# Norms that travel by rows: column sums, a power on GpSimd and a spread through device memory

## The chip, the cores and the metric

The kernel runs on one core of a Trainium2 chip. The metric is the device time of one execution in microseconds (us). Three executions of the kernel before took 1455.49, 1453.04 and 1453.77 us, so the median is 1453.77 us. A core has five engines with a queue each: TensorE (PE, matrix products; PEld is its loading of weights), VectorE (DVE), ScalarE (ACT), GpSimd (POOL) and SyncE (SP, which only issues transfers). ScalarE and GpSimd can issue transfers too. Each queue is worked off in order, and an instruction that waits holds up those behind it.

## The reference

The program is a two-layer encoder over x (512 positions of 1024 features) and a memory of 256 positions. Everything is float32.

```python
def rms_norm(x, gain):
    y = x32 * lax.rsqrt(jnp.mean(x32 * x32, axis=-1, keepdims=True) + RMS_EPS)
    return (y * gain).astype(x.dtype)
...
for layer in range(DEPTH):
    xn = rms_norm(x, mix_norm[layer])
    mixed = fox_diff_mixer(xn, ...) if layer % 2 == 0 else mlstm_mixer(xn, ...)
    x = x + mixed
    x = x + memory_cross_attention(rms_norm(x, xattn_norm[layer]), rms_norm(mem, mem_norm[layer]), ...)
    x = x + conv_ffn(rms_norm(x, ffn_norm[layer]), ...)
return rms_norm(x, final_norm)
```

Layer 0's mixer has eight heads of forgetting attention, whose logits get the running sum of a gate per key position, and four heads of differential attention, whose outputs are each normed (`rms_norm(d_out, subln)`). Layer 1's mixer is an mLSTM with four heads; a running maximum and its exponential per position enter each head, and each head's output is normed. So besides the three norms of x in each layer, the last norm and two norms of the memory, there are eight norms of heads. The two norms of the memory differ only in their gains.

## The kernel before, in words

Activations lie with features on the 128 partitions and the 512 positions along the free axis, in eight blocks. A product in full precision is made of three matmuls (`mm3`, L289 to L291, and L351 to L353 where positions become rows) on a high part in the format fp32r and a low rest. The high part is made by ScalarE (`split`, L282) and the rest by VectorE (L279). Weights come in blocks of 128x1024 by SyncE's queue into three "raw" buffers and are split into three pairs of buffers. Projections collect in four accumulator banks ("acc"); four more PSUM banks ("s" and "w", two of each) serve the rest.

A norm's gain is put on x before the projection, and its root per position after it, when the accumulator is emptied. The root is made like this. ScalarE and VectorE sum the squares of all blocks into one tile of 128x512 (`squares`). `rsqrt_cols` sums over the partitions with eight small instructions on TensorE (L417; in the feed-forward part L1218), so that position p of a group lies on partition p. `rsqrt` makes the inverse root on VectorE with a first guess from the bits and three Newton steps (L426 to L432). `bcast_cols` spreads it to all 128 partitions: VectorE multiplies a unit matrix by the high and the low part of the roots (L446), two matmuls with ones put the result into a bank (L452), and ScalarE copies it to the tile "rb" (L456), or VectorE reads it there. Gate rows of single heads are split (`split_rows`) and spread by a matmul with a selecting matrix (`bcast_row`, L612).

The order of the mixers and of cross-attention is made by a planner (`Plan`), a list by priority with a resource for each kind of buffer, and that of the feed-forward part by `Sched`, with due times; both work with assumed costs. The framework below takes their order as a priority, schedules again by its own estimates, and adds the waits. At the end of each mixer stand fill blocks (`p_fill`: two blocks of the next part's keys, each with a bank), then the output projection (`p_out`): eight projections of eight steps, where step k needs the k-th block of the mixer's output. Cross-attention (`xattn`) follows with queries from x and keys and values from the memory; its query evacuation (L1057) multiplies by rb. The feed-forward part (`ffn_steps`) begins with four pairs of plain up-projections, whose evacuation (L1317) multiplies by rb, and four blocks of transforms of x on VectorE (L1251 to L1259) for the later pairs, which are multiplied with seven products in place of eight. The last part (`finish`) norms in two halves and writes the output.

Of the kernel before, what the change touches and what calls it, by code (L numbers as in the profile page):

```python
# [16 lines left out]
P = 128  # L17
# [12 lines left out]
WARM = 12  # L30
DECAY_AT = 90.0
# [48 lines left out]
class Plan:  # L80
# [17 lines left out]
    def run(self):  # L98
        todo = sorted(self.items, key=lambda i: (i.prio, i.n))
        eng, t = self.eng, self.t  # L100
        while todo:
# [29 lines left out]
            for e, d in pick.chain:  # L131
                u = max(u, eng[e]) + d
                eng[e] = u
                u += 0.06
# [103 lines left out]
class Builder:  # L238
# [130 lines left out]
    def p_norm(self, pl, state, n, done, scale, eps, fin, deps=(), prio=None, after=0.0, fdeps=(), chain=(("A", 0.5),)):  # L369

        st = {}

        def one():
            st["r"] = self.rsqrt_cols(state["sq"], n, scale, eps)

        def two():
            fin(st["r"], self.bcast_cols(st["r"], n, *done))

        a = pl.add(one, 0.4 * n / 512, deps, prio, take=("s",), free=("s",), chain=(("D", 2.3),), after=after)
        return pl.add(two, 0.5 * n / 512, [a, *fdeps], prio, take=("s",), free=("s",), chain=chain)  # L380

    def x_norm(self, pl, prio=0, after=0.0, deps=()):
        def fin(r, rb):
            self.r, self.rb = r, rb

        return self.p_norm(pl, self.state, SEQ, (self.sp, "rb", 1), 1.0 / DM, EPS, fin, deps, prio, after)

# [32 lines left out]
    def rsqrt(self, ps, nt, scale, eps):  # L420
        nc = self.nc
        z = self.til(self.sp, "z", (P, 4))[:, :nt]
        zh = self.til(self.sp, "zh", (P, 4))[:, :nt]
        y = self.til(self.sp, "y", (P, 4))[:, :nt]
        a = self.til(self.sp, "a", (P, 4))[:, :nt]
        nc.vector.tensor_scalar(out=z, in0=ps[:, 0 : 2 * nt : 2], scalar1=float(scale), scalar2=float(eps), op0=ALU.mult, op1=ALU.add)  # L426
        nc.vector.tensor_scalar(out=y.bitcast(I32), in0=z.bitcast(I32), scalar1=-0.5, scalar2=1597463007.0, op0=ALU.mult, op1=ALU.add)
        nc.vector.tensor_scalar(out=zh, in0=z, scalar1=-0.5, scalar2=None, op0=ALU.mult)
        for _ in range(3):
            nc.vector.tensor_tensor(out=a, in0=y, in1=y, op=ALU.mult)  # L430
            nc.vector.tensor_tensor(out=a, in0=a, in1=zh, op=ALU.mult)
            nc.vector.scalar_tensor_tensor(out=y, in0=a, scalar=1.5, in1=y, op0=ALU.add, op1=ALU.mult)  # L432
        return y

    def bcast_cols(self, r, n, pool=None, tag=None, bufs=2):
# [7 lines left out]
        ps = self.bank("b")  # L443
        for i, part in enumerate((rh, rl)):
# [7 lines left out]
            nc.tensor.matmul(banked(ps[:, :n]), self.onesr[:], alternate(dg[:, :nt, :].rearrange("p a b -> p (a b)")), start=i == 0, stop=i == 1)  # L452
        if pool is None:
            return restored(ps[:, :n])
        out = self.til(pool, tag, (P, n), bufs=bufs)
        nc.scalar.copy(folded(out[:, :n]), restored(ps[:, :n]))  # L456
# [47 lines left out]
    def xnorm(self, state):  # L504
        self.r = self.rsqrt_cols(state["sq"], SEQ, 1.0 / DM, EPS)
        self.rb = self.bcast_cols(self.r, SEQ, self.sp, "rb", 1)

# [7 lines left out]
    def constants(self):  # L515
# [8 lines left out]
        self.selc = cp.tile([P, 12], F32, name="selc")  # L524
        nc.vector.tensor_tensor(out=self.selc[:, 0:8], in0=self.ident[:, 0:8], in1=self.ident[:, 32:40], op=ALU.add)
        nc.vector.tensor_tensor(out=self.selc[:, 8:12], in0=self.ident[:, 64:68], in1=self.ident[:, 96:100], op=ALU.add)
# [67 lines left out]
    def split_rows(self, pool, *rows):  # L594

        t = pool.tile([P, SEQ], F32R, name=self.nm("rows"))
        self.nc.gpsimd.memset(t[:].bitcast(F32), 0.0)
        for n, v in enumerate(rows):
            h = v.shape[0]
            hi, lo = t[64 * n : 64 * n + h, :], t[64 * n + 32 : 64 * n + 32 + h, :]  # L600
            self.nc.scalar.copy(hi, v)
            part = self.til(self.sp, "sqt")
            self.nc.scalar.copy(part[:h, :], hi.bitcast(F32))
            self.nc.vector.tensor_tensor(out=lo, in0=v, in1=part[:h, :], op=ALU.subtract)
        return t

    def bcast_row(self, rows, c):

        ps = self.bank("b")
        s = self.til(self.sp, "sel", (P, P), F32R)  # L610
        self.nc.vector.tensor_copy(s[:], self.selc[:, c : c + 1].to_broadcast([P, P]))
        self.nc.tensor.matmul(banked(ps[:]), s[:], alternate(rows[:]), start=True, stop=True)  # L612
        return restored(ps[:])

# [42 lines left out]
    def p_soft(self, pl, st, s, i, bias, deps, prio):  # L657
# [6 lines left out]
        def score():  # L664
# [6 lines left out]
            e = res["e"] = self.x[self.turns % 8]  # L671
            self.turns += 1
# [22 lines left out]
    def turn(self, e, i, pt):  # L695

        nc = self.nc
        ps = self.bank("t")
# [45 lines left out]
    def mix0(self):  # L744
        nc, t, tc = self.nc, self.t, self.tc
        with tc.tile_pool(name="mix0", bufs=1, reuse_waits="tile") as mp:
# [5 lines left out]
            NTA = 3  # L752
# [6 lines left out]
            pl = Plan(s=2, w=2, e=8, qk=2, pt=3, ta=NTA, v=2, wt=3)  # L759
            self.state = {}  # L760
            self.turns = 0
            self.xh, self.xl = [None] * 8, [None] * 8
            self.x = [self.xp.tile([P, SEQ], F32, name=f"x{k}") for k in range(KB8)]
            gw = self.gate_weights(t["gate0"], 8, [(0, 0, 40, 8)])
# [34 lines left out]

            def spread():  # L800
                self.rb = self.bcast_cols(self.r, SEQ, self.sp, "rb", 1)

            norm = pl.add(inverse, 0, [last], 0.5, free=("s",), chain=(("D", 2.3),))
            norm = pl.add(spread, 0.5, [norm], 0.5, take=("s",), free=("s",), chain=(("A", 0.5),))
# [9 lines left out]
            def decays():  # L814
                f = self.log_sigmoid_sum(rows["z"], 8, mp, "ta", "tb", "tmp", NTA)
                rows["f"] = self.split_rows(mp, f)

            g = self.p_gate(pl, lambda: gw, 40, gates, xk, [norm], 1)
            g = pl.add(decays, 0, [g], 1, take=("ta", "ta"), free=("ta", "ta"), chain=(("A", 1.0), ("D", 4.0), ("A", 1.0), ("D", 0.6)), after=DECAY_AT)
# [4 lines left out]
            for h in range(4):  # L824
# [7 lines left out]
                for i in range(4):  # L832
# [5 lines left out]
                    def both(r1=r1, r2=r2, n=n):  # L838
# [3 lines left out]
                        nc.vector.scalar_tensor_tensor(out=e1[:, :n], in0=e1[:, :n], scalar=s1[:, 2:3], in1=e2[:, :n], op0=ALU.mult, op1=ALU.add)  # L842

# [19 lines left out]
                def scaled(r, rb, h=h, o=o):  # L863
                    q = o["o"]
                    nc.vector.scalar_tensor_tensor(out=folded(q[:]), in0=folded(q[:]), scalar=sub8, in1=rb, op0=ALU.mult, op1=ALU.mult)
# [6 lines left out]
            for p_ in range(4):  # L872
# [8 lines left out]
                for s in range(2):  # L881
# [9 lines left out]
                    b = pl.add(spread, MM, [g, *qk], p + SOFT_PRIO, take=("s", "ta"), free=("s",), chain=(("A", 0.5),))  # L891
# [22 lines left out]
                pl.add(lambda: None, 0, ss, p + SOFT_PRIO, free=("qk", "ta", "ta"))  # L914
# [29 lines left out]
    def p_memory(self, pl, layer, at, step, order=()):  # L944
# [3 lines left out]
        self.memr = mp.tile([P, 2], F32, name=f"memr{layer}")  # L948
# [12 lines left out]
        for k in range(KB8):  # L961

            def prep(k=k):
# [4 lines left out]
                self.squares(k, raw, MEM, state)  # L968
# [865 lines left out]
```

## Time and profile before

| What | Value |
|---|---|
| median of three executions | 1453.77 us |
| the profiled execution, whole | 1455.27 us |
| its span in the profile | 1453.5 us |
| TensorE busy | 1427.1 us |
| VectorE busy | 1193.3 us |
| ScalarE busy | 801.7 us |
| GpSimd busy | 57.9 us |
| granted TensorE clock, mean | 0.998 |
| read from device memory, written | 168.21 MB, 2.10 MB |

The span runs from the first to the last instruction of the program; the whole time includes what lies around it. In rows of groups, the two numbers behind the bar are the group's busy time in us and the mean of one instruction in ns; then follows the idle time of the engine just before them and what ended it. In rows in order of time, the first number is the start in us and the second the length. Matmuls overlap with the ones behind them: a row's length is longer than the time from its start to the next one's. In the chain, pieces are cut so that they don't overlap. A row of a transfer has its size and the median time from issue to landing.

### The profile page before, as it was taken

Reading aid. Unit: us, or ns where it says so; the run is one execution under the profiler, and the core shown is the slowest. Engines: PE = TensorE matmul, PEld = TensorE weight load, DVE = VectorE, ACT = ScalarE, POOL = GpSimd, SP = SyncE. Lnnn points to the kernel's source line nnn. Section 1 sums busy time; section 2 is a strip of 40 time slices with the busy share of each in tenths; the row PEclk is TensorE's granted clock in tenths of the full one; section 3 lists DMA queues with packets and bytes.
Section 4 is the critical chain, followed back from the end, with each engine's and each line's share of the span. In section 5 each row is a group of like instructions: output and inputs, shape, how many; then the busy total and the mean of one; then the engine's idle time right before and its main releaser. Section 6 shows DMA issues by size and latency. Waiting matters only on the chain.

```text
span 1453.5 us, 22202 instructions
## 1 busy us (share of the span) xinstructions
PE 1427.1 (98%) x8330; PEld 1267.4 (87%) x8330; DVE 1193.3 (82%) x2255; ACT 801.7 (55%) x1345; POOL 57.9 (4%) x100
## 2 busy tenths in 40 slices
PE   9999999999999999999999999999999999999998
PEld 7888868899889999899888788889988899999987
DVE  7778886766689999999778868676667999999975
ACT  7767574444466555545456734444445655555544
POOL 0000120000001000000000100000000000000000
PEclk9999999999999999999999999999999999999999
DMA  5222304324248666542332232323323756564322
GB/s 200 88 73 73 102 32 158 117 86 131 87 138 196 172 156 166 145 131 66 94 103 87 74 102 78 111 91 127 117 87 123 200 156 168 159 160 133 89 70 80
DMA packets 60796, 171.74 MB, mean 118 GB/s; under 512 B 6673, under 2 KB 6673, under 8 KB 60689
## 3 DMA queue, kind: packets, MB, share of 16 engines
q1 hardware_dynamic: 55072, 152.43, 32.3%
q0 software_dynamic: 4608, 16.78, 6.9%
q8 instruction: 65, 1.06, 0.3%
q10 hardware_dynamic: 1008, 1.12, 0.2%
q14 instruction: 43, 0.34, 0.1%
HBM read 168.21 MB, written 2.10 MB: 117 GB/s over the span
## 4 chain that ended last, share of the span: by engine, by line
PE 68%; DVE 22%; issue 4%; ACT 4%; DMA 1%; POOL 0%; DVEq 0%; ACTq 0%; POOLq 0%
PE acc L289 13%; PE acc L291 13%; PE acc L290 13%; DVE wl L279 5%; DVE c L1281 4%; PE w L289 3%; PE w L290 3%; PE w L291 3%; PE acc L351 2%; PE s L289 2%; PE acc L352 2%; PE acc L353 2%; PE s L291 2%; PE s L290 2%; PE w L1621 1%
## 5 line engine op out<-in xcount | busy, mean ns | idle before, releaser
L289 PE MATMUL acc<-xh,wh 128*128 128x512 f32 (+1 forms) x832 | 293.3, 353 | 0.1
L291 PE MATMUL acc<-xh,wl 128*128 128x512 f32 (+1 forms) x832 | 289.1, 347 | 1.3 <-DVE wl L279 1.3
L290 PE MATMUL acc<-xl,wh 128*128 128x512 f32 (+1 forms) x832 | 289.0, 347 | 0.0
L279 DVE TENSOR_TENSOR wl<-raw,wh 128x1024 fp32r<-128x1024 f32 (+2 forms) x201 | 240.6, 1197 | 39.3 <-ACT wh L282 35.8
L282 ACT CAST wh<-raw 128x1024 fp32r<-128x1024 f32 (+2 forms) x137 | 140.3, 1026 | 156.2 <-PE acc L290 96.7
L291 PEld LDWEIGHTS acc<-xh,wl 128*128 128x128 f32 x832 | 158.2, 190 | 16.8 <-DVE wl L279 1.6
L289 PEld LDWEIGHTS acc<-xh,wh 128*128 128x128 f32 x832 | 158.2, 190 | 15.4 <-ACT v L1393 0.3
L290 PEld LDWEIGHTS acc<-xl,wh 128*128 128x128 f32 x832 | 158.2, 190 | 15.0
L1281 DVE SCALAR_TENSOR_TENSOR c<-hs,vec,c 128x512 f32<-128x512 f32 x176 | 129.3, 750 | 5.1 <-ACT c L1274 4.6
L289 PE MATMUL w<-ah,wh 128*128 128x512 f32 x304 | 115.6, 380 | 0.0
L291 PE MATMUL w<-ah,wl 128*128 128x512 f32 x304 | 115.3, 379 | 0.0
L290 PE MATMUL w<-al,wh 128*128 128x512 f32 x304 | 115.3, 379 | 0.0
L1274 ACT ACTIVATE c<-hs,vec 128x512 f32<-128x512 f32 x88 | 69.7, 812 | 56.5 <-DVE hs L1419 49.2
L291 PEld LDWEIGHTS w<-ah,wl 128*128 128x128 f32 x304 | 57.5, 189 | 8.1
L289 PEld LDWEIGHTS w<-ah,wh 128*128 128x128 f32 x304 | 57.7, 190 | 7.2 <-ACT c L1289 0.5
L290 PEld LDWEIGHTS w<-al,wh 128*128 128x128 f32 x304 | 57.7, 190 | 6.7
L289 PE MATMUL acc<-mem,wh 128*128 128x256 f32 (+1 forms) x192 | 60.3, 314 | 0.0
L291 PE MATMUL acc<-mem,wl 128*128 128x256 f32 (+1 forms) x192 | 59.8, 311 | 0.0
L290 PE MATMUL acc<-mem,wh 128*128 128x256 f32 (+1 forms) x192 | 59.6, 311 | 0.0
L512 DVE TENSOR_TENSOR x<-w,x 128x512 f32<-128x512 f32 x72 | 49.5, 688 | 9.1 <-PE w L291 9.1
L1183 ACT CAST wh<-dr 128x512 fp32r<-128x512 f32 x64 | 39.4, 615 | 31.1 <-PE w L290 15.3
L512 DVE TENSOR_TENSOR x<-acc,x 128x512 f32<-128x512 f32 x32 | 22.1, 691 | 40.4 <-PE acc L291 40.4
(373 smaller groups left out, 3758.5 us busy)
## 6 DMA issues: line engine op xcount, KB each, us to landing
raw<-in_up_dram SPq DMA_DIRECT2D x56, 512.0 KB, 3.3
dr<-in_down_dram SPq DMA_DIRECT2D x64, 256.0 KB, 2.9
sa<-in_up_dram SPq DMA_DIRECT2D x32, 512.0 KB, 4.2
sa<-in_up_dram POOLq DMA_DIRECT2D x32, 512.0 KB, 5.5
raw<-in_xk_dram SPq DMA_DIRECT2D x16, 512.0 KB, 3.3
raw<-in_wo_dram SPq DMA_DIRECT2D x16, 512.0 KB, 3.2
raw<-in_xq_dram SPq DMA_DIRECT2D x16, 512.0 KB, 3.3
raw<-in_xv_dram SPq DMA_DIRECT2D x16, 512.0 KB, 3.2
```

Source lines behind the costliest of these rows:

```text
L279: self.nc.vector.tensor_tensor(out=lo, in0=v, in1=hi.bitcast(F32), op=ALU.subtract)
L282: self.nc.scalar.copy(hi, v)
L289: mm(out, wh, xh, start=first, stop=False, skip_group_check=parts)
L290: mm(out, wh, xl, start=False, stop=False, skip_group_check=parts)
L291: mm(out, wl, xh, start=False, stop=last, skip_group_check=parts)
L351: mm(ps, xh[k][:, ts], wh, start=(k == 0), stop=False)
L352: mm(ps, xh[k][:, ts], wl, start=False, stop=False)
L353: mm(ps, xl[k][:, ts], wh, start=False, stop=(k == 7))
L512: self.nc.vector.tensor_tensor(out=x, in0=restored(ps[:]), in1=x, op=ALU.add)
L1183: nc.scalar.copy(st["wh"][:, :cols], st[tag][:, :cols])
L1274: nc.scalar.activation(st["c_"][:, j, :], hs()[:, j, 2:514], AF.Identity, scale=self.col("cw", (layer * 3 + 2) * 44 + blk), bias=self.col( ...
L1281: nc.vector.scalar_tensor_tensor(out=c, in0=hs()[:, j, n : n + 512], scalar=w, in1=c, op0=ALU.mult, op1=ALU.add)
```

## The change

Twelve norms (both of cross-attention, both of the feed-forward parts, four heads of differential attention, four of the mLSTM) take a new way, `p_row_norm`:

1. ScalarE casts the summed squares and VectorE subtracts, which gives a high and a low part (`row_parts`).
2. Two matmuls of 512 columns with the ones as weights sum over the partitions (`row_sums`); every partition then holds the whole row. ScalarE writes one partition's row, scaled and with epsilon added.
3. ScalarE's queue copies the row from one partition to 128 partitions of four values (`row_turned`).
4. GpSimd raises it to the power -0.5 and its queue stores it to a tile in device memory (`row_root`).
5. SyncE's queue loads that row into all 128 partitions (`row_spread`).

The other norms keep their way, but their root too is a power on GpSimd in place of the Newton steps, and the products with the unit matrix become a step of their own. The gate rows are stored to device memory and loaded into 128 partitions, one transfer for each forgetting head and two for each mLSTM head; the mLSTM's second row is put through the exponential before that, on four partitions. The memory's roots are made in layer 0 only, stored, and loaded again for layer 1, whose squares of the memory are dropped. Buffers: "ta" goes from three to two, the gate rows of layer 0 get three of their own ("fb"), those of layer 1 two each, and the eight tiles that hold attention scores are taken from a list of free ones. The planner gets assumed costs for transfers.

```diff
+ROW_DMA, SPREAD_DMA = 2.5, 3.1
...
+    def row_parts(self, sq):
+        hi, lo = (self.til(self.sp, "sqt", dtype=F32R) for _ in range(2))
+        self.split(hi[:], lo[:], sq[:])
+        return hi, lo
+
+    def row_sums(self, parts, scale, eps):
+        ps = self.bank("b")
+        for i, part in enumerate(parts):
+            self.nc.tensor.matmul(banked(ps[:]), self.onesr[:], alternate(part[:]), start=i == 0, stop=i == 1)
+        row = self.til(self.sp, "sqt")
+        self.nc.scalar.activation(folded(row[0:1, :]), restored(ps[0:1, :]), AF.Copy, scale=float(scale), bias=float(eps))
+        return row
+
+    def row_turned(self, row):
+        z = self.til(self.sp, "z", (P, 4))
+        self.nc.scalar.dma_start(z[:], row[0:1, :].rearrange("o (p j) -> o p j", j=4))
+        return z
+
+    def row_root(self, z):
+        y = self.til(self.sp, "y", (P, 4))
+        self.nc.gpsimd.tensor_tensor(out=y[:], in0=z[:], in1=self.power[:], op=ALU.pow)
+        d = self.til(self.dp, "roots", (1, SEQ))
+        self.nc.gpsimd.dma_start(d[:].rearrange("o (p j) -> (o p) j", j=4), y[:])
+        return d
+
+    def row_spread(self, d, to):
+        rb = self.til(*to)
+        self.nc.sync.dma_start(rb[:], d[0:1, :].to_broadcast([P, SEQ]))
+        return rb
...
     def rsqrt(self, ps, nt, scale, eps):
...
-        nc.vector.tensor_scalar(out=y.bitcast(I32), in0=z.bitcast(I32), scalar1=-0.5, scalar2=1597463007.0, op0=ALU.mult, op1=ALU.add)
-        nc.vector.tensor_scalar(out=zh, in0=z, scalar1=-0.5, scalar2=None, op0=ALU.mult)
-        for _ in range(3):
-            nc.vector.tensor_tensor(out=a, in0=y, in1=y, op=ALU.mult)
-            nc.vector.tensor_tensor(out=a, in0=a, in1=zh, op=ALU.mult)
-            nc.vector.scalar_tensor_tensor(out=y, in0=a, scalar=1.5, in1=y, op0=ALU.add, op1=ALU.mult)
+        nc.gpsimd.tensor_tensor(out=y, in0=z, in1=self.power[:, :nt], op=ALU.pow)
...
+    def spread_row(self, rows, c, tile):
+        self.nc.sync.dma_start(tile[:], rows[c : c + 1, :].to_broadcast([P, SEQ]))
...
-            NTA = 3
+            NTA = 2
...
-            pl = Plan(s=2, w=2, e=8, qk=2, pt=3, ta=NTA, v=2, wt=3)
+            pl = Plan(s=2, w=2, e=8, qk=2, pt=3, ta=NTA, fb=3, v=2, wt=3)
...
-                f = self.p_norm(pl, sq, SEQ, (), 1.0 / P, EPS, scaled, [w], p + SOFT_PRIO, chain=(("D", 0.66),))
+                f = self.p_row_norm(pl, sq, 1.0 / P, EPS, (mp, "hrb", (P, SEQ), F32, 1), scaled, [w], p + SOFT_PRIO, chain=(("D", 0.66),))
...
                     def spread(h=h, fb=fb):
-                        fps = self.bcast_row(rows["f"], h)
-                        fb["b"] = self.til(mp, "ta", bufs=NTA)
-                        nc.scalar.copy(folded(fb["b"][:]), fps)
+                        fb["b"] = self.til(mp, "fb", bufs=3)
+                        self.spread_row(rows["d"], h, fb["b"])
...
+            self.memd = self.til(self.dp, "memroots", (1, MEM), bufs=1)
+            nc.sync.dma_start(self.memd[:], rb[0:1, :])
+
+        def again():
+            self.memrb = self.til(mp, "memrb", (P, MEM), bufs=1)
+            nc.sync.dma_start(self.memrb[:], self.memd[0:1, :].to_broadcast([P, MEM]))
...
-            norm = self.x_norm(pl, 0, deps=self.xdone[7])
+            norm = self.x_row_norm(pl, 0, self.xdone[7])
...
+            a = add("ACT", 0.52, parts_, (), at)
+            a = add("DVE", 0.6, low, [a], at)
+            a = add("PE", 0.43, sums, [a], at, [("s", st)])
+            a = add("ACT", 0.6, row, [a], at, (), [("s", st)], ROW_DMA)
+            a = add("POOL", 1.05, root, [a], at, (), (), ROW_DMA)
+            return add("SP", 0.1, spread, [a], at, (), (), SPREAD_DMA)
...
-                gt["rows"] = self.split_rows(mp, mx, mt)
+                nc.scalar.activation(mt, mt, AF.Exp, scale=-1.0)
+                gt["rows"] = mx, mt
                 gt["u"] = zi
+                gt["d"] = [self.til(self.dp, n, (H, SEQ), bufs=1) for n in ("mx", "emt")]
+                for d, v in zip(gt["d"], gt["rows"]):
+                    nc.gpsimd.dma_start(d[:], v)
...
-                f = self.p_norm(pl, st, SEQ, (), 1.0 / 256, 0.0, scaled, ns, p + 3, fdeps=oe, chain=(("D", 1.32),))
+                f = self.p_row_norm(pl, st, 1.0 / 256, 0.0, (mp, "hrb", (P, SEQ), F32, 1), scaled, ns, p + 3, fdeps=oe, chain=(("D", 1.32),))
```

More of the change, by code (lines that the diff above doesn't have):

```diff
@@ L367, in p_proj_tok, with p_norm @@
         ]
[L369 removed]
+    def p_norm(self, pl, state, n, done, scale, eps, fin, deps=(), prio=None, after=0.0):
         st = {}
@@ L376, in two @@
         def two():
[L377 to L380 removed]
+            fin(st["r"], self.spread_cols(st["d"], n, *done))
+        a = pl.add(one, 0.9 * n / 512, deps, prio, take=("s",), free=("s",), chain=(("D", 0.1), ("G", 1.05)), after=after)
+        b = pl.add(lambda: st.update(d=self.diag_cols(st["r"], n)), 0, [a], prio, chain=(("D", 0.2 + 1.2 * n / 512),))
@@ L442, in bcast_cols @@
         self.sub(rl, r, rh)
-        ps = self.bank("b")
-        for i, part in enumerate((rh, rl)):
+        out = []
+        for part in (rh, rl):
             dg = self.til(self.sp, "sqt", dtype=F32R)[:].rearrange("p (a b) -> p a b", b=P)
@@ L592, in log_sigmoid_sum @@
         return f
[L594 to L613, printed above, removed]
+    def spread_row(self, rows, c, tile):
+        self.nc.sync.dma_start(tile[:], rows[c : c + 1, :].to_broadcast([P, SEQ]))
     def q_parts(self, ps):
@@ L967, in prep @@
                 raw = raws[k // 4][:, k % 4 * MEM : k % 4 * MEM + MEM]
-                self.squares(k, raw, MEM, state)
+                if layer == 0:
+                    self.squares(k, raw, MEM, state)
                 self.gained(k, raw, self.col("mem", layer * 8 + k), hi, lo)
-            done[k] = [pl.add(prep, 0, (), 0, after=at + step * (k // 4) + (k % 4) * 0.7, order=[last], chain=(("A", 0.71), ("D", 0.4)), load=(("D", 0.4),))]
+            done[k] = [pl.add(prep, 0, (), 0, after=at + step * (k // 4) + (k % 4) * 0.7, order=[last], chain=(("A", 0.71), ("D", 0.4)), load=(("D", 0.4),) if layer == 0 else ())]
         def fin(r, rb):
```

146 lines of the change are left out of this document (89 added, 57 removed).

## The prediction

> **What bounds the kernel now.** I read the page's busy line and chain first, then the waits, then busy time by stage for the first feed-forward part, then single windows around the places where a norm is made.
>
> ```profile
> span 1453.5 us, 22202 instructions
> PE 1427.1 (98%) x8330; PEld 1267.4 (87%) x8330; DVE 1193.3 (82%) x2255; ACT 801.7 (55%) x1345; POOL 57.9 (4%) x100
> PE 68%; DVE 22%; issue 4%; ACT 4%; DMA 1%; POOL 0%; DVEq 0%; ACTq 0%; POOLq 0%
> ACT wh L282 <- PE acc L290: 96.7, 40, 5.0
> core 0: us, PE busy (x) PEld busy (x) DVE busy (x) ACT busy (x) POOL busy (x), PEclk, DMA share, GB/s
> 433.00:485.00 52.00, 51.10 (x346) 47.55 (x345) 51.99 (x82) 31.44 (x49) 5.27 (x6) 1.00 0.75 189
> ```
>
> TensorE is busy for 1427.1 of 1453.5 us at a granted clock of 1.00: a matmul that goes away shortens the run, and a norm that comes late costs only where TensorE has nothing else. The fourth line says that the casts of the weights wait for TensorE to give back a buffer, so loaded weights lie ready. The row by stage shows the exception: from 433 us VectorE too is full (51.99 of 52.00), so VectorE work that starts late at the head of the feed-forward part stays late.
>
> **TensorE work.**
>
> ```profile
> L417 PE MATMUL s<-ones,sq x40: 167/251/272, 167.7 to 1445.0; 128*128 128x2 f32 x40
> L417 PE MATMUL s<-ones,tb x32: 168/251/252, 99.8 to 156.5; 128*128 128x2 f32 x32
> L417 PE MATMUL s<-ones,hsq x32: 168/251/251, 814.0 to 920.9; 128*128 128x2 f32 x32
> 267.33 1.01 PE s L417 x8
> 920.37 0.80 PE s L417 x8
> L452 PE MATMUL s<-sqt,ones 128*128 128x512 f32 x28 | 11.4, 429 | 2.9 <-DVE sqt L446 2.5
> 925.40 0.48 PE s L452
> 926.32 0.22 PE s L452
> L612 PE MATMUL s<-rows,sel 128*128 128x512 f32 x16 | 6.1, 410 | 0.1
> 780.66 0.59 PE L612 MATMUL s<-rows,sel 128*128 128x512 f32 x2
> 781.09 0.38 PE L289 MATMUL acc<-xh,wh 128*128 128x512 f32 x1
> ```
>
> Matmuls overlap, so their price is from start to start. Eight column sums take 0.80 to 1.01 us; I take 0.9, and twelve norms lose 12 x 0.9 = 10.8. Two gate rows occupy 780.66 to 781.09, 0.215 each: 16 x 0.215 = 3.4. A spread matmul takes 0.22 when nothing waits, and 2.9 us of idle over 28 adds 0.10: 24 x 0.32 = 7.7. Layer 1's memory norm (four small sums, two half spreads) is 0.6. Removed: 22.5. Added: two 512-column matmuls with the ones per norm, 24 at 0.22 to 0.32; I take 0.27, between the two, for some will wait: 6.4. **Net -16.1** (-14.8 to -17.2).
>
> **The chain of a new norm.** Squares ready, cast, subtract, two matmuls, row on ScalarE, transfer to columns, power on GpSimd, transfer to device memory, transfer back to 128 partitions.
>
> ```profile
> L1295 ACT CAST ah<-c 128x512 fp32r<-128x512 f32 x44 | 27.3, 620 | 37.2 <-DVE c L1291 37.1
> L279 DVE TENSOR_TENSOR al<-c,ah 128x512 fp32r<-128x512 f32 x44 | 30.4, 691 | 1.7 <-ACT ah L1295 1.4
> gw<-in_gate_dram ACTq DMA_DIRECT2D x2, 32.0 KB, 3.0
> out_dram<-th ACTq DMA_DIRECT2D x4, 256.0 KB, 2.4
> dr<-in_down_dram SPq DMA_DIRECT2D x64, 256.0 KB, 2.9
> x<-in_x_dram SPq DMA_DIRECT2D x16, 256.0 KB, 4.2
> sa<-in_up_dram POOLq DMA_DIRECT2D x32, 512.0 KB, 5.5
> L1238 POOL MEMSET hs<- 128x4 f32 x4 | 0.3, 102 | 332.7 <-PE w L290 332.7
> L1574 POOL TENSOR_SCALAR_AFFINE_SELECT mk<-mxb 128x512 f32<-128x512 f32 x4 | 4.4, 1096 | 13.4 <-ACT mxb L1557 13.4
> ```
>
> Cast 0.62, subtract 0.69, matmuls 0.44, row at most a cast's 0.62: 2.4. The trace has no transfer of 2 KB. To columns: 2.4 (shortest on ScalarE's queue) to 3.0; I take 2.4, since nothing is read from device memory. The power was never run: 0.1 (a fill of 128x4) to 1.1 (a mask of 128x512); I take 0.8, as it is arithmetic. Roots out by GpSimd: 2.4 (a store) to 5.5 (GpSimd's own accumulating load); I take 2.9, nearer the store, which moves in the same direction. Back to 128 partitions: 256 KB on SyncE's queue, 2.9 to 4.2; I take 2.9, the row with 64 samples. Seven handovers at 0.1 add 0.7. **Chain C = 12.1 us** (10.9 to 17).
>
> The Trainium skill, DMA: Bandwidth & Descriptors (Anatomy of one DMA), gives about 2.0 us fixed plus bytes at 436 GB/s per transfer. By that estimate the three trips are 6.6 instead of 8.2, and by the sums below the kernel would land near 1441.
>
> **Where the chain is on the path.**
>
> ```profile
> 917.66 0.70 DVE L1626 TENSOR_TENSOR hsq<-hsq,th 128x512 f32<-128x512 f32 x1 [1.47 <-ACT th L1625]
> 921.02 0.46 PE L289 MATMUL acc<-mixed,wh 128*128 128x512 f32 x1
> 926.57 1.41 DVE L1634 SCALAR_TENSOR_TENSOR num<-num,vec,s 128x512 f32<-128x512 f32 x2 [0.62 <-PE s L452]
> 929.27 1.29 DVE L279 TENSOR_TENSOR v<-num,v 128x512 fp32r<-128x512 f32 x2
> 407.43 0.68 DVE L486 TENSOR_TENSOR sq<-sq,sqt 128x512 f32<-128x512 f32 x1
> 416.67 0.58 ACT L456 COPY rb<-s 128x512 f32<-128x512 f32 x1 [4.41 <-PE s L452]
> 418.49 1.22 DVE L279 TENSOR_TENSOR wl<-raw,wh 128x1024 fp32r<-128x1024 f32 x1
> 266.55 0.69 DVE L486 TENSOR_TENSOR sq<-sq,sqt 128x512 f32<-128x512 f32 x1
> 274.55 0.69 DVE L1057 SCALAR_TENSOR_TENSOR tmp<-acc,rb 128x512 f32<-128x512 f32 x1 [1.19 <-ACT rb L456]
> 286.03 0.27 PE L289 MATMUL s<-kth,qh 128*128 128x256 f32 x1
> 1445.33 0.16 DVE L426 TENSOR_SCALAR z<-s 128x2 f32<-128x2 f32 x1 [0.76 <-PE s L417]
> 1447.29 0.16 DVE L432 SCALAR_TENSOR_TENSOR y<-a,y 128x2 f32<-128x2 f32 x1
> raw<-in_xq_dram SPq DMA_DIRECT2D x16, 512.0 KB, 3.3
> L282 ACT CAST wh<-raw 128x1024 fp32r<-128x1024 f32 x127 | 132.4, 1045 | 145.4 <-PE acc L290 87.5 <-PE acc L353 24.8 <-issue 24.6
> ```
>
> *End of layer 1's mixer.* The last head's squares are ready at 918.36 (917.66 + 0.70). Its output goes into steps 6 and 7 of every output projection. Two fill blocks hold two of the four accumulator banks, so before it arrives TensorE has two projections of six steps: 2 x 6 x 3 x 0.215 = 7.7 us from 921.02, less 0.4 for the shorter sums: until 928.4. Now its first low part is there at 929.9 (half of the pair at 929.27), 3.35 after the norm is used at 926.57: no gap. After: 918.4 + 12.1 + 3.35 = 933.8, **+5.4**, moving one for one with C.
>
> *Head of each feed-forward part.* Squares ready at 408.11, spread roots at 417.25. After: 420.2, 2.95 later. Only the weight subtraction at 418.49 (1.22) can go ahead meanwhile; the second block of transforms uses the buffer of the first evacuation. So VectorE, full behind this point, starts 1.75 late: **+3.5** over two layers. The products with the unit matrix and the dozen tiny steps that go from VectorE lay in this wait and relieve nothing later.
>
> *Head of each cross-attention part.* Squares at 267.24 plus 12.1 is 279.3; the query needs up to 4.8 more (274.5 to 279.3 now): 284.1, where scores start at 286.03 less 1.3 for matmuls gone: 284.7. **0**, and one for one above C of about 13.
>
> *Tail.* The root's vector chain of 2.1 us (1445.33 to 1447.45) becomes 0.16 + 0.8 + 0.2: **-0.9** (-0.6 to -1.6 between the ends of the power).
>
> **Edits at nothing.** The diff heads' four norms and the first three mLSTM heads' are consumed by the output projections, tens of us later; the shorter "ta" pool (three to two) is covered as gate rows leave it. Gate rows are loaded ahead, hidden by the query and key projections. The store and reload of the memory roots, and layer 1's dropped squares, lie beside full TensorE work. Longer waits on GpSimd's queue delay the masks (L900, L1574) and the accumulating loads (L1336) queued behind; GpSimd is busy 4%. ScalarE's queue gains a store behind its own row. On SyncE's queue each spread stands among weight loads, which three raw buffers keep ahead of TensorE; if that cover were gone, one would cost a load of about 3.3, a cast of 1.05 and a subtraction of 1.22: 5.6.
>
> **Sum.** -16.1 + 5.4 + 3.5 - 0.9 = **-8.1**. The profiled execution took 1455.27 (1.8 around the span), 1.5 above the median of 1453.77; on the median this gives **1445.7**. With C from 10.9 to 13.4 it is 1442 to 1450: the likeliest case's own range.
>
> **Rivals.** *All hidden:* the order moves fill work into the three gaps and only TensorE's saving shows: 1453.8 - 17.0 = 1436.8. For it: projections, fills and values can be shifted. Against: two banks and VectorE's full 52 us are limits that order doesn't lift.
>
> *Slow trips, slower than before:* the stalls grow with C once in the mixer, twice in feed-forward and, above 13.1, twice in cross-attention. At 13.1 the sum is -5.1, and five per us above: zero at C = 14.1, 0.2% slower at 14.7. At 17 it is +14.5: 1468. For it: the 5.5 and 4.2 rows, and three queues each shared with other work. Against: all rows beside 2.4 and 2.9 move far more bytes or read device memory. The Trainium skill, DMA: Bandwidth & Descriptors (Specifications), says transfers below 512 B are read, modified and written; the pieces here are 16 B, and that would push this way. The gate weights, whose pieces are 256 B, landed in 3.0 against 2.9 for 2 KB pieces, so the trace shows next to no penalty.
>
> *Queue blocked:* a spread whose roots come later than the order assumed holds the weights behind it, 5.6 each at worst; three such give the gain back, five make 1466. For it: 28 new transfers wait on SyncE's queue. Against: the fourth line of the first fence.
>
> **How the numbers follow.** Forecast 0.50; all hidden 0.17; C of 13.5 to 14.7, about no change, 0.13; slow trips 0.14; queue blocked 0.06. About 0.2%, 2.9 us, is what a measurement can tell. Faster 0.67, same 0.13, slower 0.20. The range reaches from the hidden case, 1436, into the slow one, 1459.
>
> **What would show it.** TensorE busy near 1411; no matmul of the gate rows; 24 sums of 512 columns; a TensorE gap of about 5 us before steps 6 and 7 of layer 1's output projection; the feed-forward's first evacuation about 3 us later against its squares; scores of cross-attention without a gap. Wrong if squares-to-spread takes over 14 us, if weight casts begin to wait for transfers, or if GpSimd's power takes several us.

## The result and the profile after

The changed kernel takes 1467.70 us (median of five executions, 1467.64 to 1468.26), the kernel before 1453.77 beside it: the ratio is 1.0095, with a 95% interval of 1.0084 to 1.0106. It is slower by 13.9 us, where 1445.7 was forecast. The profiled execution's span grew by 12.4 us.

From the page of the kernel after, and then its view of cores (span and mean granted clock):

```profile
span 1465.9 us, 21753 instructions
PE 1416.2 (97%) x8212; PEld 1259.2 (86%) x8212; DVE 1146.7 (78%) x1976; ACT 799.9 (55%) x1335; POOL 88.0 (6%) x130
```

```profile
core 0: 1465.9 us, clock 0.994
```

TensorE lost 118 matmuls and 10.9 us of busy time, and VectorE 46.6 us, as the change promised; yet the span grew. VectorE is idle more, not busier, and the mean clock fell from 0.998 to 0.994. The view of waits names what stood still: first VectorE, then TensorE. In each row stands the waiting engine, tile and line, what it waited for, the sum in us, how often, and the longest.

```profile
DVE num L1702 <- DMA hrb<-roots: 13.0, 3, 6.9
DVE tmp L1115 <- DMA rb<-roots: 12.5, 2, 6.5
DVE ta L913 <- DMA hrb<-roots: 8.0, 3, 3.9
DVE hs L1388 <- DMA rb<-roots: 7.8, 2, 3.9
```

```profile
PE acc L356 <- DVE wl L283: 5.7, 2, 3.1
PE s L1648 <- ACT k L1603: 5.6, 3, 3.0
PE s L295 <- DVE wl L283: 4.3, 2, 2.2
PE acc L293 <- ACT v L286: 4.1, 1, 4.1
```

VectorE stands for 41.3 us in front of spread roots that have not landed. Of TensorE's new waits only the fourth is for an output of a norm (`v`, the last mLSTM head's). The others are for: low parts of weights (`wl`), the mLSTM's keys (`k`). They lie in VectorE's queue behind the instruction that waits, or need one that does. The order of time at the head of layer 0's cross-attention shows it (start, length, engine, line; in brackets the idle time before and what ended it):

```profile
265.17 0.48 ACTq L426 DMA_DIRECT2D z<-sqt  x1
268.57 1.01 POOL L431 TENSOR_TENSOR y<-z,power 128x4 f32<-128x4 f32 x1 [59.29 <-DMA z<-sqt]
269.88 0.61 POOL L433 DMA_DIRECT2D roots<-y  x1 [0.29 <-POOL y L431]
271.64 0.33 SPq L438 DMA_DIRECT2D rb<-roots  x1
275.89 0.38 PE L355 MATMUL acc<-wh,mem 128*128 128x512 f32 x1
276.39 1.29 DVE L1115 SCALAR_TENSOR_TENSOR tmp<-acc,rb 128x512 f32<-128x512 f32 x2 [5.98 <-DMA rb<-roots]
277.60 1.22 DVE L283 TENSOR_TENSOR wl<-raw,wh 128x1024 fp32r<-128x1024 f32 x1
278.87 0.48 PE L356 MATMUL acc<-wl,mem 128*128 128x512 f32 x1 [2.60 <-DVE wl L283]
```

The scaling of the first query (L1115) heads VectorE's queue and waits 5.98 us for the spread. Behind it stands the subtraction of a weight block for the memory's values, which has nothing to do with the norm. TensorE uses up the high part and stands from 276.1 to 278.9.

By part of the program (a part ends where the last residual addition of its output starts, the first mixer begins at 0), in us; the third kernel, in which nothing waits for the new norms, is explained below:

| Part | before | after | difference | after, no norm awaited |
|---|---|---|---|---|
| mixer, layer 0 | 263.5 | 257.5 | -6.0 | 254.3 |
| cross-attention, layer 0 | 141.2 | 142.8 | +1.6 | 139.9 |
| feed-forward, layer 0 | 337.3 | 340.4 | +3.1 | 337.0 |
| mixer, layer 1 | 222.2 | 227.6 | +5.4 | 219.0 |
| cross-attention, layer 1 | 141.2 | 145.0 | +3.8 | 139.9 |
| feed-forward, layer 1 | 305.4 | 309.6 | +4.2 | 309.1 |
| rest | 42.7 | 43.0 | +0.3 | 42.6 |

### The profile page after: what moved, and what is told of

Same layout as the page of the kernel before. It is cut to its first block, busy times and chain, and to the rows that moved or that the text cites. A ratio compares the mean times of both kernels' runs of the same rounds, so it can differ in the third digit from the quotient of the medians.

```text
span 1465.9 us, 21753 instructions
## 1 busy us (share of the span) xinstructions
PE 1416.2 (97%) x8212; PEld 1259.2 (86%) x8212; DVE 1146.7 (78%) x1976; ACT 799.9 (55%) x1335; POOL 88.0 (6%) x130
```

## The experiments

Theory V was formed from the rows above: an instruction that waits for the spread roots stands at the head of VectorE's queue, and TensorE runs dry of what lies behind it. Its rivals were Q, spreads that hold up weights on SyncE's queue, and O, an order of the work that the planner made worse.

**Norms by columns again, one group at a time.** The edits put the old way back (with the power on GpSimd for the root), first for each group alone, then for all three:

```diff
-            norm = self.x_row_norm(pl, 0, self.xdone[7])          # x_cols
+            norm = self.x_norm(pl, 0, deps=self.xdone[7])
-            a = add("ACT", 0.52, parts_, (), at) ...              # f_cols
+            a = pe(0.5, sums, (), [("s", st)]) ...
-                f = self.p_row_norm(pl, st, 1.0 / 256, ...)       # h_cols
+                f = self.p_norm(pl, st, SEQ, (mp, "hrb", 1), 1.0 / 256, ...)
```

> The changed kernel, with the norms of the two cross-attention parts made by columns again (column sums, power on GpSimd, spread by TensorE). Theory V (VectorE takes its queue in order, and the first use of the spread roots stands at its head until the transfer lands, with weight subtractions that TensorE needs behind it): the 7.2 us that TensorE lost in the two cross-attention parts (2.5 and 4.7) come back, less 2 x 0.9 of matmuls: 1462. Theory Q (the spreads hold up the weight loads on SyncE's queue everywhere): 2 of some 20 spreads go, about a tenth of the loss: 1466. Theory O (the planner's new order of the work lost the time, not the norms' length): 1468, no change.

> The changed kernel, with the norms of the two feed-forward parts by columns again. Theory V: the 9.1 us that TensorE lost in the two feed-forward parts (4.0 and 5.1) come back, less 1.8 of matmuls: 1460. Theory Q: 1466. Theory O: 1468.

> The changed kernel, with the norms of layer 1's four mLSTM heads by columns again. Theory V: the 12.9 us that TensorE lost in that mixer come back, less 4 x 0.9 of matmuls: 1458; 1462 if the three small gaps between 765 and 800 us have another cause than the heads' norms. Theory Q: 4 of some 20 spreads go: 1465. Theory O: 1468.

> All three together: cross-attention, feed-forward and mLSTM heads by columns, and only the four diff heads by rows; gate rows by DMA and one memory norm stay. Theory V: the three gains add up, 1467.7 - 29.2 + 7.2 = 1446, below the kernel before (1453.8). Theory Q: 8 of some 20 spreads go: 1462. Theory O: above 1454.

Measured, against the kernel before (1.0095 for the whole change): cross-attention by columns 1.0053 (1.0038 to 1.0068), 1462.0 us; feed-forward 1.0058 (1.0035 to 1.0081); mLSTM heads 1.0088 (1.0070 to 1.0106); all three 1.0003 (0.9994 to 1.0013), 1454.8 us. So cross-attention gives back 6.1 us, near V's 5.7. The feed-forward parts give back 5.4 (2.0 to 8.7 by the interval), between V's 7.7 and Q's 1.7. The heads give back only 1.0 where V asked for 5.7 to 9.7, which is nearer to O's nothing. In that kernel's profile layer 1's mixer does shrink by 3.0 us (227.6 to 224.6), but parts that the edit does not touch grow (layer 0's mixer from 257.5 to 259.4, the cross-attention parts by 1.2 and 1.0): an edit also moves time in parts that it leaves alone. All three give back 13.4 of the 22 that V asked for and stay above 1454, as O said. V names the places in cross-attention and feed-forward, but columns with the power on GpSimd are not as cheap as the old columns, and layer 1's mixer (224.6 us in the third and fourth kernel, 222.2 before) holds something else too.

**What the old columns with a power still cost, and layer 1's gate rows.** In the first kernel Newton's root is put back on VectorE; in the next two, layer 1's gate rows are spread by TensorE again, with the power and with Newton's root:

```diff
-        nc.gpsimd.tensor_tensor(out=y, in0=z, in1=self.power[:, :nt], op=ALU.pow)      # newton
+        nc.vector.tensor_scalar(out=y.bitcast(I32), in0=z.bitcast(I32), ...)  # and three Newton steps
-                        self.spread_row(gt["d"][i], h, st[n])                          # rows_mm, newton_mm
+                    mxp = self.bcast_row(gt["rows"], h)
```

> The kernel with cross-attention, feed-forward and mLSTM heads by columns (1454.8), and Newton's root on VectorE in place of the power on GpSimd in all norms by columns. If the wait of VectorE for GpSimd's power (10.1 us over ten norms) is what the feed-forward parts still lose (1.9 and 2.6 us against before): 1450. If it is the order of the work: 1455.

> The kernel with cross-attention, feed-forward and mLSTM heads by columns (1454.8), and layer 1's gate rows spread by TensorE as before, with the due times that went with it. If the gate rows by DMA are what opened the gaps at 762, 782, 796 and 886 us (layer 1's mixer is 2.4 us longer than before although its matmuls are 4.0 us less): the mixer goes back to 222 and the kernel to 1452. If they are not: 8 matmuls more, 1.7 us: 1456.5.

> The kernel with Newton's root that was faster than before (diff heads by rows, gate rows by DMA, one memory norm), with layer 1's gate rows spread by TensorE again and their due times. If those due times are what keeps layer 1's mixer 1.7 us longer than before: the mixer takes 222 and the kernel is 1 to 2 us faster than with gate rows by DMA. If not: 1.7 us slower, by 8 matmuls.

Measured: 0.9975 (0.9965 to 0.9985) with Newton's root, 1.0013 (1.0003 to 1.0022) with the gate rows by TensorE, 0.9980 (0.9971 to 0.9989) with both. The power on GpSimd costs the columns 0.0028, 4.1 us, as expected in size, but not because the norm is longer. In layer 0's feed-forward part the first scaled accumulator comes 7.2 us after the squares with the power (401.67 to 408.86) and 9.2 with Newton's root (401.24 to 410.41), and the part is still some 3 us shorter with Newton's (335.9 against 339.2). So it is not the length of the norm that decides there. What is left is the order in which the framework puts the instructions by its own estimates; no run tests that alone. Layer 1's gate rows by DMA are no loss: taking them back brings nothing that is clear of the intervals, and the mixer stays at 224 to 225.

The kernel with Newton's root stands below the kernel before and the changed one: diff heads by rows, both layers' gate rows by DMA, one memory norm, all else by columns as before. 0.9975 is 3.6 us faster than before.

**Only what touches layer 0 and the memory,** on the kernel before:

```diff
+                f = self.p_row_norm(pl, sq, 1.0 / P, EPS, (mp, "hrb", (P, SEQ), F32, 1), scaled, [w], p + SOFT_PRIO, ...)
+                        self.spread_row(rows["d"], h, fb["b"])
+        if layer: self.memnorm = pl.add(again, 0, done[7], 1, chain=(("-", SPREAD_DMA),)); return
```

> The kernel before, with only three parts of the change: the norms of the four diff heads by rows, layer 0's gate rows by DMA, one memory norm for both layers. Everything else as before (Newton's root on VectorE, columns, layer 1's gate rows by TensorE). Theory V (the removed matmuls pay in full where no instruction stands and waits on TensorE's path): layer 0's mixer gains the 6.0 us that it gained in the changed kernel, layer 1's memory norm 0.6: 1453.8 - 6.6 = 1447. Theory O (each such edit makes the planner lose about as much elsewhere): 1452 to 1455.

Measured 0.9992 (0.9983 to 1.0001): 1.2 us of the 6.6, not clear of zero, and the number that theory O gave. The mixer gained 2.9, not 6.0. The order of time of this kernel shows where time goes:

```profile
173.69 0.75 DVE L930 SCALAR_TENSOR_TENSOR ta<-ta,warm,hrb 128x512 f32<-128x512 f32 x1 [3.50 <-DMA hrb<-roots]
176.99 0.17 DVE L499 CAST rh<-y 128x2 fp32r<-128x2 f32 x1
177.74 0.92 PE L510 MATMUL s<-sqt,ones 128*128 128x256 f32 x2 [3.32 <-DVE sqt L504]
```

A diff head's scaling waits 3.50 us for its spread, and the memory's norm, made by columns, has its Newton steps behind it; TensorE stands 3.32 us for a product of that other norm, and its granted clock is 0.50 from 176.62 to 183.45, which loses up to 3.4 us more (last section). So even a norm whose own result is needed tens of us later costs time, by what is queued behind its first use.

**How long the spread takes, and what a longer chain costs.** Two kernels change only the transfers of the twelve norms:

```diff
-        self.nc.sync.dma_start(rb[:], d[0:1, :].to_broadcast([P, SEQ]))
+        self.nc.sync.dma_start(rb[:], d[:])                                            # plain: 128 rows
+        self.nc.sync.dma_start(rb[:], d[:].unsqueeze(1).to_broadcast([8, 16, SEQ]))    # rows8
```

> The changed kernel, with the spread reading 128 different rows of device memory (256 KB, of which the first row is the roots and the others are rows of x) in place of one row 128 times; so 127 of 128 partitions are scaled with wrong numbers. If reading one row 128 times is what makes the spread 4.8 us long: it lands in about 3, and the two feed-forward and two cross-attention parts and the end of layer 1's mixer gain up to 1.9 each: 1458 to 1460. If 256 KB take that long in this place whatever they are: 4.8 again, and 1468.

> The changed kernel; GpSimd stores the roots eight times, in eight rows of device memory, and the spread reads each row 16 times in place of one row 128 times. If reading one row again and again is what makes the spread slow (128 different rows landed in 3.3 to 3.7 where one row took 4.1 to 4.8): between the two, 1460 to 1464, unless the longer store (1024 pieces of 16 bytes in place of 128) gives it back. If not: 1468 or more.

The rows of transfers (kernel after, then the one with 128 different rows; the last number is the median from issue to landing in us):

```profile
hrb<-roots SPq DMA_DIRECT2D x8, 256.0 KB, 4.1
rb<-roots SPq DMA_DIRECT2D x4, 256.0 KB, 4.8
z<-sqt ACTq DMA_DIRECT2D x12, 2.0 KB, 2.3
roots<-y POOLq DMA_DIRECT2D x12, 2.0 KB, 1.8
```

```profile
hrb<-plain SPq DMA_DIRECT2D x8, 256.0 KB, 3.3
rb<-plain SPq DMA_DIRECT2D x4, 256.0 KB, 3.7
```

Reading one row 128 times takes about 1 us longer than reading 128 rows of the same size, and that is not all of the difference to 2.9. The kernel with 128 rows stands at 1.0040 (1.0026 to 1.0054), 8.0 us better. With eight rows the spread was used 4.2 us after its issue at the head of layer 0's feed-forward part, against 5.0, but the store took 3.5 us instead of 1.8, the chain grew by about 1 us, and the kernel stands at 1.0175 (1.0160 to 1.0191), 11.6 us worse. Both ways, 1 us of chain in twelve norms moves the end by about 10 us. Much of that is the slow clock of the last section: by the traces' clock records, stretches at half clock cost at most 4.8 us with 128 rows, 10.0 in the kernel after and 21.0 with eight rows.

**What stands behind, and SyncE's queue.** In the next three kernels the first tells the planner longer transfers, so that the uses are put later; the second lets GpSimd issue the spreads; the third plans the mLSTM heads' norms ahead of all else:

```diff
-ROW_DMA, SPREAD_DMA = 2.5, 3.1                          # told
+ROW_DMA, SPREAD_DMA = 3.2, 4.8
-        self.nc.sync.dma_start(rb[:], ...)              # gp_spread
+        self.nc.gpsimd.dma_start(rb[:], ...)
-                                    ... scaled, ns, p + 3, fdeps=oe, ...     # heads_first
+                                    ... scaled, ns, 0, fdeps=oe, ...
```

> The changed kernel; only the two constants from which the order is planned are other: 3.2 us for each short transfer and 4.8 for the spread (2.5 and 3.1 in the change), so that what uses the spread roots is put later in VectorE's queue. No operation is added or removed. Theory V (instructions behind the standing one lose the time): TensorE's gap in layer 1's mixer at 886 us (3.2) and those in cross-attention (2.8 and 3.3) shrink or go: 1460 to 1464. Theory Q or a loss by the length of the chain alone: 1468.

> The changed kernel; GpSimd issues the spread too, so no spread stands on SyncE's queue (SyncE waited 45 us in 12 places for the roots to be stored). Theory Q (weights behind a waiting spread come late): faster, by up to the 5.6 us per place of the prediction: 1455 to 1462. Theory V: GpSimd's own transfers have been no shorter than SyncE's: 1467 to 1470.

> The changed kernel; the norms of layer 1's mLSTM heads are planned ahead of all other work, so that the sums of the squares don't stand behind other matmuls (at the last head they ran 5.5 us after their operands were there, and SyncE issued the spread 3.5 us after the store where 1.8 is possible). If that is what made the last head's chain 18.3 us and not 12.1 to 13.6: TensorE's gap of 4.3 us at the end of the mixer and the slow clock behind it go, 1462 to 1464. If the gap comes from elsewhere: 1467.

Measured: 1.0078 (1.0063 to 1.0093) when told, 2.5 us better than the change, with the gaps of cross-attention down from 2.8 and 3.3 us to 1.8 and 2.6 and that at 886 us from 3.2 to 2.3: the right way, but at the low end of what V asked for: VectorE's waits for spreads fell only from 41.3 to 37.4 us, as the uses moved little. Layer 0's mixer took 2.8 us back (260.3 for 257.5): TensorE has a new gap of 4.4 us there, ended at 165.78, with a granted clock of 0.50 from 165.17 to 171.99. With GpSimd's spreads 1.0190 (1.0173 to 1.0207), 13.8 us worse, and VectorE's waits for spreads stayed at 41.7 us. That is no sign of Q, but it does not settle Q either, for this kernel adds a loss of its own:

```profile
PE s L293 <- ACT wh L1420: 9.6, 4, 4.8
```

These waits for weight casts of the feed-forward parts are 2.1 us in the kernel after; GpSimd's queue accumulates some of those blocks, and ScalarE waits 8.4 us for them here. Heads first, 1.0090 (1.0066 to 1.0114), changed nothing that can be told: the last head's row began 5.5 us after the end of the subtraction, as before. Why its sums are placed so late is not settled.

**Nothing waited for.** Every operation stays, but each spread reads the roots of the norm before, most of which have long been stored:

```diff
+        self.past.append(d)
+        d = self.past[max(0, len(self.past) - 2)]
         self.nc.sync.dma_start(rb[:], d[0:1, :].to_broadcast([P, SEQ]))
```

> The changed kernel; each spread reads the roots of the norm before (long stored) in place of its own, so every operation of the chain still runs but nothing waits for it. The output is scaled with wrong roots. If the waits for the chain are the whole loss: every stage falls to its TensorE work, and the time goes to the prediction's case with all hidden, 1437 to 1441; cross-attention to about 139.8 us each, the feed-forward parts 4 to 5 us shorter each, layer 1's mixer about 10 us shorter. What stays above that in a stage is a loss by the order of the work (theory O), not by the norm's length.

Measured 0.9903 (0.9885 to 0.9921): 14.1 us faster than before and 27.9 faster than the change. The table above has its parts. Cross-attention falls to 139.9 as expected. This kernel's waits, VectorE's for the spreads and then two of TensorE's:

```profile
DVE ta L916 <- DMA hrb<-roots: 3.5, 2, 3.2
DVE num L1705 <- DMA hrb<-roots: 3.5, 1, 3.5
```

```profile
PE s L1651 <- ACT k L1606: 2.5, 2, 1.6
PE s L1574 <- DVE cv L1559: 1.5, 1, 1.5
```

41.3 us of waiting became 7.0, and the loss turned into a gain. What is left, 7.0 us, belongs to the first norm, which here reads its own roots, and to heads that follow the one before them closely. That is the loss in one number: the waits for the new norms cost about 28 us, some 6 of them through the slow clock (last section), and the work taken off the engines is worth 14. The framework can also put these spreads elsewhere in its order (that of layer 0's feed-forward norm is issued at 347.39, 50 us before the norm begins), so a share of the order in the 28 is not excluded. Layer 1's feed-forward part stays long here (309.1) in part because of a weight transfer that landed late in this one execution and cost a gap of 2.2 us and, by half clock behind it, 1.7 more. Layer 1's mixer keeps waits for the gates (`cv`) and keys (`k`), from which V can't free it: 3.2 us of gain for about 6.3 us of matmuls removed (by the prediction's prices: four norms at 1.0, eight gate rows at 0.215, the memory's norm at 0.6). Why these points of wait did not come earlier with less work ahead of them stays open; the gate rows are not the reason.

## Why the prediction was wrong

By the prediction's own prices (a norm 1.0, a gate row 0.215, the memory's norm 0.6, stalls of +5.4 and twice +1.75) the parts should have changed by -5.7, -1.0 and +0.8 us in layer 0 and by -0.9, -1.0 and +0.8 in layer 1. They changed by -6.0, +1.6 and +3.1, and by +5.4, +3.8 and +4.2. So cross-attention misses by 7.4 us, layer 1's mixer by 6.3 and the feed-forward parts by 5.8, nearly all of the difference. That layer 1's mixer changed by just the +5.4 forecast for its gap is chance.

**TensorE work, -16.1: right.** 24 sums of 512 columns are there (20 at L419, four in the feed-forward parts), no matmul of a gate row is, and with the waits gone TensorE's busy time fell by 17.7 us (1427.1 to 1409.4) and the kernel gained 14.1 us (11.5 to 16.7 by the interval), a little less than the 17.0 of this term and the tail's. In the changed kernel the TensorE busy time of 1411 was missed (1416.2), among other things because matmuls behind a gap run at half the clock (last section).

**Chain C, 12.1 us: too short, by the spread first.** At the head of layer 0's feed-forward part, where nothing else disturbs it:

```profile
403.94 0.61 ACT L1275 CAST sqt<-sq 128x512 fp32r<-128x512 f32 x1
407.33 0.48 ACTq L426 DMA_DIRECT2D z<-sqt  x1
409.39 1.04 POOL L431 TENSOR_TENSOR y<-z,power 128x4 f32<-128x4 f32 x1 [41.49 <-DMA z<-sqt]
410.72 0.61 POOL L433 DMA_DIRECT2D roots<-y  x1 [0.29 <-POOL y L431]
412.50 0.33 SPq L438 DMA_DIRECT2D rb<-roots  x1
417.54 1.29 DVE L1388 TENSOR_TENSOR hs<-acc,rb 128x512 f32<-128x512 f32 x2 [3.90 <-DMA rb<-roots]
```

13.6 us from the cast to the use. The row of columns took 2.06 (2.4 taken), the power 1.04 (0.8 taken), the store 1.78 (2.9 taken), the spread 5.04 (2.9 taken), and cast to issue 3.39 with its handovers (2.4 taken). The Trainium skill, DMA: Bandwidth & Descriptors (Anatomy of one DMA), with its fixed 2.0 us, came close for the two short transfers (2.06 and 1.78) and not for the spread. The page gives that figure for GpSimd's path, and the prediction put it to all three queues. In cross-attention C was 15.1 and 15.6: the row's transfer, issued 0.2 us after a weight load of 512 KB (264.97 and 265.17 in layer 0), took 3.4. At layer 1's last head it was 18.3. So in the feed-forward part C lay in the case of "about no change", and in cross-attention and at the last head in the rival "slow trips", to which 0.14 was given; at 14.7 that rival was to begin losing.

**Head of the feed-forward parts, +3.5: too small.** In the profile the parts grew by 3.1 and 4.2 although about 1.0 of matmuls went from each. The mechanism was right (VectorE is full and starts late), the delay was 4.5 instead of 2.95, and little of it was covered. A part of this may belong to the order, as the kernels with Newton's root suggest.

**Heads of cross-attention, 0: wrong step.** The margin was counted to the scores, along the query's own path. What ran out first was the low part of a weight block, queued behind the use (276.39, 277.60 and 278.87 above). The waits cost 2.9 and 5.1 us there. By the prediction's own rule, one for one above 13.1, the measured C of 15.1 and 15.6 would have made 2.0 and 2.5.

**End of layer 1's mixer, +5.4: near in size, by other terms.** The gap before steps 6 and 7 is there (4.3 us, and slow matmuls behind it), but the squares were ready 7 us earlier than assumed and the chain took 6 longer, so two errors cancelled by luck. Against the chain of 13.6 above, cast to issue took 7.5 us in place of 3.4 (the sums ran at 917.03, 4.5 us after the subtraction that they need had ended), the store 1.7 more and the spread 1.1 less.

**"Edits at nothing" for the other seven head norms: the step that failed most plainly.** Their outputs are indeed needed late, but their first use stands in VectorE's queue. In layer 1's mixer:

```profile
883.32 0.75 DVE L1702 SCALAR_TENSOR_TENSOR num<-num,vec,hrb 128x512 f32<-128x512 f32 x1 [3.02 <-DMA hrb<-roots]
885.32 1.53 DVE L1598 SCALAR_TENSOR_TENSOR cv<-hs,vec,cv 128x512 f32<-128x512 f32 x2
889.21 0.63 ACT L1603 ACTIVATE k<-cv 128x512 f32<-128x512 f32 x1 [1.10 <-DVE cv L1601]
889.89 0.70 PE L1648 MATMUL s<-q,k 128*128 128x512 f32 x1 [3.00 <-ACT k L1603]
```

VectorE waits 3.02 us for a head's roots; the next head's convolution, and with it the keys, come 3 us late, and TensorE stands 3.00. I asked who needs the result and not who stands behind the first reader; the zero for cross-attention comes from the same question. With the waits gone, layer 0's mixer was 3.2 us shorter and layer 1's 8.6.

**Queue blocked: no sign of it.** SyncE's queue waited for roots, but waits of weight casts for transfers are not among ScalarE's long ones (3.8 us for the down-projections' blocks, and 4.7 in the kernel that waits for no norm), and taking the spreads off that queue brought nothing, in a run with a loss of its own. The rival's price was also added up wrongly: three places of 5.6 give back -16.1, but two give back the sum of -8.1, and five would have made 1473.7.

**Tail, -0.9: right where it was put, and not seen at the end.** From the root's first step to its use 2.22 us became 0.97 (1457.61 to 1458.58), but from that use to the end of the span 5.9 became 7.3. What lengthened it is open.

## What to carry to other kernels

A wait has three prices: the path from it to the end, all that is queued behind the first instruction that waits on its in-order engine, and, after some gaps, the slow clock. To cost a longer latency, list for each use which instructions stand behind it and which engine runs dry first; "needed tens of us later" says nothing on that. A chain of several transfers is worth it only where its first use can stand in the queue behind enough other work, and each microsecond of it is then counted once per use, not once in all.

## What had not been expected

After some gaps TensorE's clock fell to half for 3.41 us. The windows of the kernel after around the gap at the end of layer 1's mixer and around the one in layer 1's cross-attention (from and to in us, length, busy time and instructions of each engine, then the granted clock, the DMA share and GB/s):

```profile
core 0: us, PE busy (x) PEld busy (x) DVE busy (x) ACT busy (x) POOL busy (x), PEclk, DMA share, GB/s
930.00:932.00 2.00, 0.00 (x0) 0.00 (x0) 2.00 (x4) 0.50 (x1) 0.00 (x0) 1.00 0.00 0
932.00:934.00 2.00, 1.83 (x5) 1.22 (x6) 1.36 (x3) 0.72 (x2) 0.00 (x0) 0.64 0.04 8
934.00:936.00 2.00, 2.00 (x6) 1.59 (x5) 0.00 (x0) 0.14 (x1) 0.00 (x0) 0.51 0.00 0
936.00:938.00 2.00, 1.86 (x9) 1.31 (x8) 1.78 (x3) 2.00 (x3) 0.00 (x0) 1.00 0.00 0
988.00:990.00 2.00, 0.00 (x0) 0.00 (x0) 2.00 (x3) 1.58 (x3) 0.00 (x0) 1.00 0.11 45
992.00:994.00 2.00, 2.00 (x6) 1.55 (x6) 1.59 (x2) 0.38 (x1) 0.00 (x0) 0.50 0.59 207
```

3.41 us at half the clock lose 1.7 us, on top of gaps of 4.3 and 3.3. The length of one gap does not decide alone: the gaps of 2.8 us at 275.9 and 3.2 us at 886.5 were followed by a full clock, those of 2.2 us before 447.08 and 1160.04 by a half one. The trace's clock records show what does: the four falls begin at 447.87, 932.57, 990.59 and 1161.26 us, and these starts lie 142, 17 and 50 times 3.413 us apart. The clock changes in steps of a fixed length, so what counts is how long TensorE idles within one step. The steps at the first of these falls and at the two harmless gaps, in the same columns:

```profile
273.80:277.21 3.41, 2.47 (x12) 1.82 (x10) 0.82 (x2) 0.04 (x1) 0.00 (x0) 1.00 0.92 216
277.21:280.62 3.41, 1.75 (x8) 1.57 (x9) 3.41 (x5) 3.01 (x4) 0.00 (x0) 1.00 0.27 85
444.46:447.87 3.41, 1.23 (x9) 1.04 (x10) 3.41 (x6) 2.38 (x4) 0.02 (x1) 1.00 0.56 178
447.87:451.28 3.41, 3.41 (x19) 3.41 (x18) 3.41 (x7) 2.81 (x5) 0.82 (x1) 0.50 0.76 185
884.78:888.19 3.41, 2.11 (x10) 1.51 (x8) 3.38 (x5) 1.23 (x2) 0.00 (x0) 1.00 0.00 0
888.19:891.61 3.42, 1.72 (x5) 0.97 (x6) 2.70 (x6) 1.25 (x2) 0.00 (x0) 1.00 0.45 153
```

The two harmless gaps lie across a border of steps and leave at most 1.70 us idle in one of them; the steps before the four falls were idle for 2.18, 3.02, 2.99 and 2.17 us. In the 16 profiles of this case, leaving out the first 6 us of each, a step at full clock with more than 2.0 us idle was always followed by half clock and one with less than 1.3 never; between the two, both occur.

The Trainium skill, TensorE: Matmul & The Clock Gate (HAM oscillation — how this bites in real kernels), tells of such a fall where TensorE idles through a window of about 3.4 us; a fall to half and a step of that length are what these rows show, but an idle time of that length is not needed: 2.18 us was enough. Over the span, the mean clock of 0.994 against 0.998 before is worth some 6 us, and 0.998 came back when nothing waited for the norms.

GpSimd's store of 128 pieces of 16 bytes took only 1.8 us, less than the 2.3 of the transfer that turns the row, and reading one row of device memory 128 times cost about 1 us more than reading 128 rows.
